# Expert 0's token rows and gates by one-hot products on TensorE, in a two-layer decoder trunk

## The chip, the core and the metric

The kernel runs on one core of one Trainium2 chip. The metric is the device time of one launch in microseconds (us); lower is better. Durations below are those of one profiled execution. Engines are named as in the profile: PE is the matmul engine (PEld its weight loads), DVE, ACT and POOL are the vector, scalar and GpSimd engines, and SP issues DMAs.

## The reference

A trunk of two layers works on 512 tokens of 1024 numbers in float32. Each layer is an attention mixer followed by a mixture of experts, and the change lies in the second part alone:

```python
def hier_moe(xn, ...):            # xn: the stream, normalised
    g_prob = softmax(xt @ w_group + b_group);  g_val, g_idx = top_k(g_prob, 1)
    e_logits = (xt @ w_expert + b_expert)[the chosen group]      # 4 of 16 experts
    e_val, e_idx = top_k(softmax(e_logits), 2);  e_val /= sum(e_val)
    gates[token, expert] = g_val * e_val                         # 0 for all others
    for e in range(16):
        hid = silu(xt @ w_gate[e]) * (xt @ w_up[e])
        out = out + gates[:, e:e + 1] * (hid @ w_down[e])
```

Every token goes to two of sixteen experts, so an expert sees some 64 of the 512 tokens. Its weights are 6 MB: `w_gate` and `w_up` of 1024x512, `w_down` of 512x1024.

## The kernel before

**Precision.** Matmul operands are split into a high and a low part of a shorter float type (`fp32r` in the profile), and a product is three matmuls, high by high, high by low and low by high (`mm3`, L480). ACT writes the high part (`wh`, L191) and DVE the low part (`wl`, L193); some low parts go to POOL. A matmul with both operands in plain float32, such as the one with `twice` in `route_lt` (L827), needs no parts.

**Weight stream.** `Stream` (L115) loads the experts' weights with one DMA of 1 MB per unit from SP's queue. An expert has six units: two of `w_gate`, two of `w_up`, two of `w_down`. Fifteen buffers take turns; a buffer comes free when both of its splits (128x1024 each) are done, and a load also waits until the load three before it has landed. The last two of the fifteen buffers are `h0` and `h1`, in which the stream of token rows `h` stood until the experts began: `row(t)` (L376) is the 128 tokens of tile `t`, `t` = 0 to 3, two tiles to a buffer. Split parts go into six pairs `wh`, `wl`; a pair comes free when the last matmul that reads it is done. `ws.get()` hands out the next pair and splits ahead as far as pairs are free; `ws.get(False)` does not split ahead; `ws.split()` makes one split; `ws.hold()` stops the loads and `ws.go()` lets them go on.

**Routing.** When attention ends, each tile's rows are multiplied by the gain and written to `xn_d` in DRAM (`route_rows`), transposed and multiplied by the routers' weights (`route_logits`, `route_lt`). `select` (L848) works on two tiles at a time (`TS` = 2): DVE compares logits (`beat`, `above`, `ab`), PE counts with `ab` how many tokens stand before each one in its expert's list (`pk`, L881), and DVE forms the place of each token in its two lists (`rs`). `make_lists` (L1278) compares places with slot numbers 1 to 96 (`oneh`, L1284), multiplies by token numbers on PE (`pi`, L1287) and has in `first` and `lists` the token number of each of an expert's 96 slots. `rest` (L915) makes the gate values `ga2` by some 17 small DVE operations and two exponentials, and writes them to `g_d` in DRAM.

**Experts.** `gather` (L1297) fetches an expert's rows from `xn_d` by an indirect DMA that POOL issues, `gates` (L1373) its gate values and row roots from `g_d`. `gathered_t` (L1303) transposes the 96 rows on PE and splits them into `th` and `tl`. `gate_up` (L1309) makes `pg` and `pu`, 24 matmuls of 128x512 each; expert 0's `pg` first takes all 16 matmuls of `th` and then the 8 of `tl`. SiLU and product give `sg`; `hidden_t` transposes and splits it; `down` multiplies by `w_down`, scales by the gates and adds the result into DRAM by an indirect DMA. The two buffers for gathered rows are `xg`.

**Order.** A scheduler orders each engine's instructions by its own estimate of times; the text of the kernel binds it by `behind(lasts)` (L299), which puts everything issued inside behind a named instruction of the same engine, without a wait. Before the change the order at the head of the experts is: `make_lists`, the gathers of experts 0 and 1, 30 matmuls without use (`warm`, L553), all of `rest`, the gates of 0 and 1, four splits, `gathered_t(0)`, gather and gates of expert 2, more splits, and then the loop over the experts.

## Time and profile before

| what | value |
|---|---|
| three timed runs | 1280.27, 1281.66, 1283.16 us (median 1281.66) |
| the profiled execution | 1280.31 us, of which 1278.3 us are the span from the first instruction to the last |
| PE busy | 1213.9 us (95%) |
| DVE, ACT, POOL busy | 1011.3 us (79%), 930.6 us (73%), 366.4 us (29%) |
| TensorE's granted clock, mean | 0.966 of full speed |
| HBM read and written | 260.35 MB, 21.83 MB |

The experts of layer 0 run from about 310 to 600 us and those of layer 1 from about 970 to 1260 us. The granted clock has two levels in this trace, 1.0 (2.4 GHz) and 0.5 (1.2 GHz). A busy PE is not a PE at its peak, since matmuls are pipelined and their ends are modelled; the distance between the starts of two matmuls says more than the duration of one.

### The profile page before, as it was taken

What the parts mean: (1) busy time and instruction counts of PE and PEld (TensorE: products, weight loads), DVE (VectorE), ACT (ScalarE), POOL (GpSimd) and SP (SyncE); (2) the same over time, 40 slices, a digit from 0 to 9 for tenths busy, and PEclk for the clock granted to TensorE, in tenths of its full rate; (3) what the DMA queues carried; (4) which work ended last, traced back from release to release, by engine and by line L of the source; (5) the groups of instructions that cost most, each with busy time, mean ns of one, the idle gap of its engine ahead of it and who ended that gap; (6) DMA issues with size and microseconds to landing.
All of it is one profiled execution on the core that took longest, in us unless ns stands there. A gap on an engine that the chain in (4) does not pass through costs nothing. (4 is left out here: it accounts for less than half of the span.)

```text
span 1278.3 us, 21170 instructions
## 1 busy us (share of the span) xinstructions
PE 1213.9 (95%) x7552; PEld 998.0 (78%) x7552; DVE 1011.3 (79%) x1828; ACT 930.6 (73%) x1697; POOL 366.4 (29%) x337
## 2 busy tenths in 40 slices
PE   8999999997999999999999999997897999999993
PEld 8999999866677777766999999997675777777762
DVE  5678889888998889887767777666587988988883
ACT  6477777655888888877667787767465888888782
POOL 2644441145113433411200011001163133343400
PEclk9999999988999999999999999998697999999997
DMA  6343324859999999995853333337459999999991
GB/s 218 92 106 78 99 59 151 264 183 298 338 349 345 332 331 332 335 350 160 246 144 87 88 100 100 86 103 240 145 190 302 357 346 319 326 322 329 332 357 23
DMA packets 167813, 286.36 MB, mean 224 GB/s; under 512 B 19876, under 2 KB 53807, under 8 KB 167700
## 3 DMA queue, kind: packets, MB, share of 16 engines
q1 hardware_dynamic: 149716, 253.60, 59.1%
q0 software_dynamic: 16496, 30.19, 11.2%
q8 instruction: 63, 1.03, 0.3%
q10 hardware_dynamic: 1488, 1.13, 0.3%
q14 instruction: 50, 0.41, 0.1%
HBM read 260.35 MB, written 21.83 MB: 221 GB/s over the span
## 5 line engine op out<-in xcount | busy, mean ns | idle before, releaser
L193 DVE TENSOR_TENSOR wl<-raw,wh 128x1024 fp32r<-128x1024 f32 (+1 forms) x390 | 472.3, 1241 | 68.1 <-ACT wh L191 64.7
L191 ACT ACTIVATE wh<-raw 128x1024 fp32r<-128x1024 f32 (+1 forms) x456 | 440.7, 988 | 84.9 <-PE pu L483 23.3
L193 POOL TENSOR_TENSOR wl<-raw,wh 128x512 fp32r<-128x512 f32 (+1 forms) x66 | 109.4, 1661 | 184.4 <-ACT wh L191 174.1
L482 PE MATMUL pj<-wl,bh 128*128 128x256 f32 x512 | 145.8, 285 | 0.0
L483 PE MATMUL pj<-wh,bl 128*128 128x256 f32 x512 | 145.6, 286 | 0.0
L481 PE MATMUL pj<-wh,bh 128*128 128x256 f32 x512 | 145.5, 286 | 0.0
L481 PE MATMUL pj<-wh,ah 128*128 128x256 f32 x384 | 110.9, 289 | 1.3 <-ACT wh L191 0.8
L482 PE MATMUL pj<-wl,ah 128*128 128x256 f32 x384 | 111.0, 289 | 1.2 <-POOL wl L193 0.9
L483 PE MATMUL pj<-wh,al 128*128 128x256 f32 x384 | 110.3, 288 | 0.0
L481 PE MATMUL pu<-wh,th 128*96 128x512 f32 x256 | 101.7, 397 | 4.0 <-ACT wh L191 4.0
L482 PE MATMUL pu<-wl,th 128*96 128x512 f32 x256 | 102.5, 400 | 0.0
L481 PE MATMUL pd<-wh,hh 128*96 128x512 f32 x256 | 102.2, 399 | 0.0
L483 PE MATMUL pu<-wh,tl 128*96 128x512 f32 x256 | 101.2, 395 | 0.0
L482 PE MATMUL pd<-wl,hh 128*96 128x512 f32 x256 | 101.1, 395 | 0.0
L483 PE MATMUL pd<-wh,hl 128*96 128x512 f32 x256 | 101.1, 395 | 0.0
L482 PEld LDWEIGHTS pj<-wl,bh 128*128 128x128 f32 x512 | 97.9, 191 | 0.1
L481 PEld LDWEIGHTS pj<-wh,bh 128*128 128x128 f32 x512 | 97.6, 191 | 0.1
L483 PEld LDWEIGHTS pj<-wh,bl 128*128 128x128 f32 x512 | 97.7, 191 | 0.0
L483 PE MATMUL pg<-wh,tl 128*96 128x512 f32 x240 | 97.5, 406 | 0.0
L481 PE MATMUL pg<-wh,th 128*96 128x512 f32 x240 | 96.2, 401 | 0.0
L482 PE MATMUL pg<-wl,th 128*96 128x512 f32 x240 | 95.9, 400 | 0.2 <-DVE wl L193 0.2
L1298 POOL DMA_INDIRECT xg<-xn_d,lists x28 | 50.8, 1813 | 104.1 <-PE xt L527 104.1
(386 smaller groups left out, 2945.7 us busy)
## 6 DMA issues: line engine op xcount, KB each, us to landing
raw<-in_moe_w_gate_dram SPq DMA_DIRECT2D x64, 1024.0 KB
raw<-in_moe_w_up_dram SPq DMA_DIRECT2D x64, 1024.0 KB
raw<-in_moe_w_down_dram SPq DMA_DIRECT2D x64, 1024.0 KB
raw<-in_kv_w_dram SPq DMA_DIRECT2D x12, 1024.0 KB
raw<-in_a_w_in_dram SPq DMA_DIRECT2D x11, 1024.0 KB
raw<-in_b_w_q_dram SPq DMA_DIRECT2D x6, 1024.0 KB
kh<-kh POOLq DMA_DIRECT2D x24, 128.0 KB, 2.9
kl<-kl POOLq DMA_DIRECT2D x24, 128.0 KB, 2.8
```

Source lines behind the costliest of these rows:

```text
L191: nc.scalar.activation(hi[:, o:o + n], src, AF.Copy)
L193: e.tensor_tensor(lo[:, o:o + n], src, hi[:, o:o + n].bitcast(F32), op=ALU.subtract)
L481: nc.tensor.matmul(o, lh, rh, start=start, stop=False)
L482: nc.tensor.matmul(o, lh, rl, start=False, stop=False)
L483: nc.tensor.matmul(o, ll, rh, start=False, stop=stop)
L1298: nc.gpsimd.indirect_dma_start(out=xg[e % XG], out_offset=None, in_=xn_d, in_offset=bass.IndirectOffsetOnAxis(ap=(first if e < XG else lis ...
```

## The change

Expert 0 is no longer gathered from DRAM. For each tile a 0/1 matrix `pick` (128 tokens x 96 slots, float32) is made on DVE from the place of each token in expert 0's list (`rk0`), and plain float32 matmuls `row(t)` by `pick` give the transposed rows of the 96 slots in two banks `picked[0]` and `picked[1]`, each of four 128x96 blocks that sum over the four tiles: 32 products. Eight of them (tiles 0 and 1, first bank) stand behind 24 matmuls without use and ahead of `pk` of the second two tiles; eight (tiles 0 and 1, second bank) behind that `pk`; sixteen (tiles 2 and 3) behind `make_lists`. The split scales by the gain column for column. Expert 0's gate values come out of `ga2` in the same way, by four products (`picked_gates`). Its low part `tl0` takes the buffer `yb` in which results stand later, and `pick` a buffer of `hh`.

The loads into `h0` and `h1` move behind these products, the hold on the loads is gone, and the gathers of experts 1 and 2 follow `make_lists`. `rest` is cut into two pieces that stand between splits, each split and each piece behind the DVE operation before it (`chain`). Expert 0's `pg` takes its eight blocks in two halves and releases two weight pairs after each half; SiLU of expert 0, its transposition and the gates of experts 1 and 2 come later than before.

```diff
-WARM = 60, 30, 20
+WARM = 60, 24, 20
@@ select
-        for t in range(t0, t1):
-            o = pk[:, (t - t0) * 16:(t - t0) * 16 + 16]
+        with behind(r["early"]() if t0 else {}):
+            for t in range(t0, t1):
...
+        r["pkm"] = marks()[mybir.EngineType.PE]
+        with tc.high_priority(100):
+            nc.vector.scalar_tensor_tensor(r["rk0"][:, t0:t1], pk[:, 0:n * 16].rearrange("p (t e) -> p t e", e=NE)[:, :, 0],
+                                           1.0, ab[:, t0:t1, 0], op0=ALU.add, op1=ALU.mult)
@@ rest: yields after the two exponentials and after the write of g_d
+            yield
+            cmax = kt([1, 1], "cmax")
...
@@ moe
-            with behind({sp.engine: sp}, r["sp"]):
-                for i in range(2):
-                    ws.ring(f"h{i}", ...)
-            ws.hold()
+            pick = pm.tile([P, NT, CAP], F32, tag="hh", name="pick", bufs=2)
+            picked = []
+            def pick_ones(t0):
+                with tc.high_priority(100):
+                    for t in range(t0, t0 + TS):
+                        nc.vector.tensor_scalar(pick[:, t], slot16[:, 0:CAP], r["rk0"][:, t:t + 1], None, op0=ALU.is_equal)
+            def pick_rows(t0, gs):
+                for g, k in itertools.product(gs, range(4)):
+                    kc = g * 4 + k
+                    for t in range(t0, t0 + TS):
+                        nc.tensor.matmul(picked[g][:, k * CAP:(k + 1) * CAP], row(t)[:, kc * P:(kc + 1) * P], pick[:, t],
+                                         start=t == 0 and k == 0, stop=t == NT - 1 and k == 3)
+                return marks()[mybir.EngineType.PE]
+            def early():
+                pe = marks()[mybir.EngineType.PE]
+                with behind({pe.engine: pe}):
+                    warm(WARM[1], "pj")
...
+                with behind({pe.engine: pe}):
+                    return {pe.engine: pick_rows(0, [0])}
+            r["early"] = early
+            pick_ones(0)
             route(layer)
+            pick_ones(TS)
+            pe = r["pkm"]
+            with behind({pe.engine: pe}):
+                pe = pick_rows(0, [1])
@@ expert 0's operands and gates
+            def picked_t():
+                th = pm.tile([P, KC, CAP], F32R, tag="th", name="th0", bufs=2)
+                tl = pm.tile([P, KC, CAP], F32R, tag="yb", name="tl0", bufs=1)
+                for g in range(2):
+                    split2s([(th[:, g * 4 + k], tl[:, g * 4 + k], picked[g][:, k * CAP:(k + 1) * CAP],
+                              gffn[layer][:, g * 4 + k:g * 4 + k + 1]) for k in range(4)])
+                    dve = marks()[mybir.EngineType.DVE]
+                    with behind({dve.engine: dve}):
+                        ws.split()
+                return th, tl
+            def picked_gates():
+                pt = ps("sc", "pgx")[0:CAP, 0:NE + 1]
+                for t in range(NT):
+                    nc.tensor.matmul(pt, pick[:, t], r["ga2"][:, t], start=t == 0, stop=t == NT - 1)
+                nc.vector.tensor_copy(gx[0], pt)
@@ gate_up, expert 0
-                        w = [ws.get() for _ in range(4)]
-                        for k in range(2):
-                            for kc in range(KC):
+                        for g in range(2):
+                            w = [ws.get(False) for _ in range(2)]
+                            for k, kc in itertools.product(range(2), range(g * 4, g * 4 + 4)):
...
+                        amid()
@@ the order at the head
-            make_lists()
-            for i in range(XG):
-                gather(i)
-            ws.go(marks()[mybir.EngineType.DVE].name, last_unit[layer] + 1)
...
+            with behind({pe.engine: pe}):
+                make_lists()
             pe = marks()[mybir.EngineType.PE]
             with behind({pe.engine: pe}):
-                warm(WARM[1], "pj")
...
+                pick_rows(TS, range(2))
+            with behind({sp.engine: sp}, r["sp"]):
+                for i in range(2):
+                    ws.ring(f"h{i}", ...)
+            ws.go(None, last_unit[layer] + 1)
+            for i in (1, 2):
+                gather(i)
+            rest = r["rest"]()
...
+            with behind({**r["lsm"], dve.engine: dve}):      # dve: the second oneh
+                for _ in range(2):
+                    ws.split()
+            dve = r["lim"]                                   # lists
+            with behind({dve.engine: dve}):
+                chain(ws.split, also=r["lsm"])
+                tt = picked_t()
+            chain(ws.split, lambda: next(rest), also=r["lsm"])
...
+                    banks = gate_up(0, *tt, lambda: chain(ws.split, ws.split))
+                    chain(lambda: next(rest), ws.split)
...
+                    chain(second_in, first_gates, ws.split)  # gathered_t(1), picked_gates
...
+                    with behind(dve):
+                        sg = activate(0, *banks)
+                        make_last()
+                    for i in (1, 2):
+                        gates(i)
+                    gather(3)
+                    gates(3)
```

## Rows read from the trace of the kernel before

**Rows 1.** Windows, layer 0's head and its steady part; the header names the columns.
```profile
core 0: us, PE busy (x) PEld busy (x) DVE busy (x) ACT busy (x) POOL busy (x), PEclk, DMA share, GB/s
...
299.90:306.70 6.80, 4.42 (x47) 4.23 (x47) 5.76 (x38) 3.85 (x6) 1.98 (x2) 0.51 0.71 240
...
310.12:313.55 3.43, 3.43 (x8) 2.32 (x9) 3.43 (x5) 0.33 (x1) 3.40 (x1) 0.52 0.93 134
...
324.10:326.10 2.00, 0.02 (x1) 0.00 (x0) 2.00 (x4) 2.00 (x4) 0.00 (x0) 1.00 1.02 329
...
327.20:330.60 3.40, 3.40 (x10) 2.21 (x9) 2.49 (x3) 1.28 (x2) 0.00 (x0) 0.51 1.03 323
...
340.00:560.00 220.00, 220.00 (x1050) 156.28 (x1049) 194.78 (x190) 186.50 (x224) 79.22 (x47) 1.00 1.02 338
```

**Rows 2.** Timeline of PE, layer 0: start us, length us, instruction, [idle before <-releaser].
```profile
301.35 0.17 PE L881 MATMUL pk<-ab,strictb 128*128 128x16 bf16 x1
...
303.20 3.36 PE L557 MATMUL warm<-onesb 128*128 128x128 bf16 x30
...
308.99 0.88 PE L527 MATMUL xt<-cm,xg 96*128 96x96 f32 x8 [2.34 <-DMA xg<-xn_d,first]
310.12 0.74 PE L1319 MATMUL pg<-wh,th 128*96 128x512 f32 x1 [0.25 <-ACT th L487]
...
333.19 0.39 PE L483 MATMUL pg<-wh,tl 128*96 128x512 f32 x1
```

**Rows 3.** Timeline of PE, layer 1, the same places.
```profile
960.15 0.17 PE L881 MATMUL pk<-ab,strictb 128*128 128x16 bf16 x1 [0.17 <-DVE ab L875]
...
970.03 0.74 PE L1319 MATMUL pg<-wh,th 128*96 128x512 f32 x1
...
985.52 0.47 PE L481 MATMUL pu<-wh,th 128*96 128x512 f32 x1 [2.01 <-ACT wh L191]
...
992.58 0.39 PE L483 MATMUL pg<-wh,tl 128*96 128x512 f32 x1
```

**Rows 4.** Timeline of POOL, layer 0: gathers of expert 0 and expert 2.
```profile
304.42 1.11 POOL L1298 DMA_INDIRECT xg<-xn_d,first  x1 [8.71 <-DMA raw<-in_moe_w_down_dram]
...
310.14 4.28 POOL L1298 DMA_INDIRECT xg<-xn_d,lists  x1 [3.34 <-PE xt L527]
```

**Rows 5.** Timeline of DVE, layer 0: second one-hot, first six low parts.
```profile
302.24 0.56 DVE L1284 TENSOR_TENSOR oneh<-slot,rs 128x384 f16<-128x384 f16 x1
...
306.62 2.36 DVE L193 TENSOR_TENSOR wl<-raw,wh 128x1024 fp32r<-128x1024 f32 x2
...
308.98 4.61 DVE L193 TENSOR_TENSOR wl<-raw,wh 128x1024 fp32r<-128x1024 f32 x4
313.52 1.00 DVE L488 TENSOR_TENSOR tl<-xt,th 128x384 fp32r<-128x384 f32 x2
```

**Rows 6.** Timeline of PEld: weight loads of plain float32 matmuls, 128 columns each.
```profile
297.69 0.52 PEld L827 LDWEIGHTS lt<-twice,ls 40*128 40x128 f32 x4 [0.62 <-ACT ls L823]
```

**Rows 7.** Timeline of PE: one plain float32 product of 384 columns.
```profile
69.73 0.91 PE L754 MATMUL br<-boh 33*128 33x384 f32 x2
```

**Rows 8.** Groups of DVE by shape: names, shapes, count | busy us, mean ns | idle before.
```profile
L498 DVE SCALAR_TENSOR_TENSOR al<-xt,gcols,ah 128x128 fp32r<-128x128 f32 x32 | 8.7, 342 | 6.1 <-ACT ah L496 6.1
...
L1515 DVE TENSOR_SCALAR ohlast<-slot,last 96x128 fp32r<-96x128 f16 x4 | 1.0, 351 | 0.0
```

**Rows 9.** Timeline of SP: load into `h0` in layer 0, last loads of both layers.
```profile
296.12 0.59 SPq L165 DMA_DIRECT2D raw<-in_moe_w_up_dram  x1
...
569.05 8.46 SPq L165 DMA_DIRECT2D raw<-in_moe_w_down_dram  x4
...
1230.81 8.45 SPq L165 DMA_DIRECT2D raw<-in_moe_w_down_dram  x4
```

**Rows 10.** Timeline of ACT: splits near the end of each layer's experts.
```profile
582.97 5.79 ACT L191 ACTIVATE wh<-raw 128x1024 fp32r<-128x1024 f32 x6
...
1242.21 5.79 ACT L191 ACTIVATE wh<-raw 128x1024 fp32r<-128x1024 f32 x6
```

More of the change, by code (lines that the diff above doesn't have):

```diff
@@ L877, in select @@
         pk = ps(("pv", "sc")[t0 > 0], f"pk{layer}_{t0}")
-        for t in range(t0, t1):
-            o = pk[:, (t - t0) * 16:(t - t0) * 16 + 16]
-            for u in range(t + 1):
-                nc.tensor.matmul(o, strictb if u == t else onesb, ab[:, u, :], start=t == t0 and u == 0,
-                                 stop=t == t1 - 1 and u == t)
+        with behind(r["early"]() if t0 else {}):
+            for t in range(t0, t1):
+                o = pk[:, (t - t0) * 16:(t - t0) * 16 + 16]
+                for u in range(t + 1):
+                    nc.tensor.matmul(o, strictb if u == t else onesb, ab[:, u, :], start=t == t0 and u == 0,
+                                     stop=t == t1 - 1 and u == t)
+        r["pkm"] = marks()[mybir.EngineType.PE]
+        with tc.high_priority(100):
+            nc.vector.scalar_tensor_tensor(r["rk0"][:, t0:t1], pk[:, 0:n * 16].rearrange("p (t e) -> p t e", e=NE)[:, :, 0],
+                                           1.0, ab[:, t0:t1, 0], op0=ALU.add, op1=ALU.mult)
         for k in range(2):
@@ L1285, in make_lists, with make_last @@
                                             r["rs"][:, :, t:t + TS, None].to_broadcast(shape), op=ALU.is_equal)
+                r["ohm"] = marks()[mybir.EngineType.DVE]
                 for i, (t, k) in enumerate(itertools.product(range(NT), range(2))):
                     nc.tensor.matmul(pi, oneh[:, k, t, :], r["mv"][:, k, t, :], start=i == 0, stop=i == 2 * NT - 1)
-                nc.vector.tensor_scalar(first[:, 0:XG], pi[:, 0:XG], OOB, S - 1.0, op0=ALU.add, op1=ALU.min)
+                nc.vector.tensor_scalar(first, pi[:, 0:XG + 1], OOB, S - 1.0, op0=ALU.add, op1=ALU.min)
                 nc.vector.tensor_scalar_add(lists, pi, OOB)
+                r["lim"] = marks()[mybir.EngineType.DVE]
+                r["pi"] = pi
+            def make_last():
                 if layer == 0:
@@ L1299, in gather @@
                     out=xg[e % XG], out_offset=None, in_=xn_d,
-                    in_offset=bass.IndirectOffsetOnAxis(ap=(first if e < XG else lists)[:, e:e + 1], axis=0),
+                    in_offset=bass.IndirectOffsetOnAxis(ap=(first if e <= XG else lists)[:, e:e + 1], axis=0),
                     bounds_check=S - 1, oob_is_err=False)
@@ L1389, in moe @@
-            dve = marks()[mybir.EngineType.DVE]
-            for i in range(XG):
-                gates(i)
-            with behind({**r["lsm"], dve.engine: dve}):
-                for _ in range(4):
-                    ws.split()
-            tt = gathered_t(0)
-            gather(2)
-            gates(2)
-            with behind({**r["lsm"], dve.engine: dve}):
-                ws.ahead()
+                pick_rows(TS, range(2))
+            with behind({sp.engine: sp}, r["sp"]):
+                for i in range(2):
+                    ws.ring(f"h{i}", lambda u, i=i: px.tile([P, 2048], F32, tag=f"h{i}", name=f"raw{u}"), 1)
@@ new lines, in moe, with chain @@
+            ws.go(None, last_unit[layer] + 1)
+            for i in (1, 2):
+                gather(i)
+            rest = r["rest"]()
+            def chain(*fs, also={}):
+                for f in fs:
+                    dve = marks()[mybir.EngineType.DVE]
+                    with behind({**also, dve.engine: dve}):
+                        f()
+            dve = r["ohm"]
+            with behind({**r["lsm"], dve.engine: dve}):
+                for _ in range(2):
+                    ws.split()
@@ L1409, in moe @@
                     tt = gathered_t(e + 1)
-                if hprev is not None:
-                    down(e - 1, *hprev)
+                down(e - 1, *hprev)
                 if e + 3 < NE:
```

59 lines of the change are left out of this document (37 added, 22 removed).

## Prediction

> **What bounds the kernel now.** I read the windows first. Through the experts of a layer PE has no idle time: 220.00 of 220 us between 340 and 560 [rows 1]. There the kernel moves at PE's pace, and what the change can win lies at the two heads, before that state is reached. The same view shows what a head loses: the clock stands at about half from 299.90 to 306.70 and again from 310.12 to 313.55, PE does nothing from 324.10 to 326.10, and the clock is at half once more from 327.20 to 330.60 [rows 1]. The timeline of PE names the waits. After the last count `pk` at 301.35 PE has only lists and matmuls without use to do until expert 0's rows have landed; they are transposed at 308.99 and the first matmul of the experts starts at 310.12 [rows 2]. Layer 1 repeats it: `pk` at 960.15, first matmul at 970.03, and a stall of 2.01 us that a high part from ACT ends at 985.52 [rows 3]. So a head lasts from `pk` to the end of expert 1's `pg`: 301.35 to 333.4 (last start 333.19) and 960.15 to 992.8 [rows 2, 3], about 32 us each. From there on I let everything shift rigidly, unless the weight stream objects.
>
> **The change part by part (layer 0's times).**
>
> *Price of a product.* The trace before has no float32 product of 96 columns, so I bound it. A plain float32 matmul is two instructions, each with its own weight load. Four such loads take 0.52 us at the full clock [rows 6]; with some 0.18 for the last that is (0.52 - 0.18) / 3 = 0.11 us from load to load. The product of 384 columns takes 0.91 us as two instructions [rows 7], 1.2 ns a column and instruction at most, and 0.8 if one load of 0.11 and a tail of some 0.17 are taken off; for 96 columns that is 0.08 to 0.11 us. The load is the longer part, so an instruction costs 0.11 us and a product 0.22; the lower bound is 0.16 (streaming alone), the upper 0.44 (everything at half clock). I take 0.22, since the clock must fall for the other end. The Trainium skill, FP8 and Floating Point Precision, TensorE Precision Notes, counts a true float32 product as four passes through the array. By that rule alone a product of 96 columns would be an estimated 0.16 us and the start below would come 1 us earlier; the rows with their loads decide.
>
> *Up to the first matmul.* The matmuls without use, 30 in 3.36 us at half clock (0.11 each) [rows 2], become 24 and move to 298.3, right after the last logits, where the clock is still full: 0.055 each, 1.3 us, to 299.6. The first `pk` and, on DVE, `rk0` and two comparisons of 128x96 (0.25 each from the four of `ohlast` in 1.0 us [rows 8]) bring the first eight products to 300.6. They take 1.8 us, and the second `pk` stands behind them: 302.4 instead of 301.35, a wait that the change adds. From `pk` to the end of the second one-hot DVE took 302.80 - 301.35 = 1.45 us [rows 2, 5]; `rk0` and two comparisons add 0.7, so the one-hot ends at 304.6, and the next eight products are hidden beside it on PE (302.7 to 304.5). `pi` costs 0.5 us, then sixteen products 3.6: PE is free for experts at 308.7. The first bank is complete at 306.9 and its four high parts cost ACT 1.1 us (as DVE's 128x128 pieces, four in 8.7 / 32 x 4 = 1.1 [rows 8]), so they are no later. Start 308.7 against 310.12: 1.4 us gained. Layer 1 has the same path from a `pk` 658.8 us later, so 967.5 against 970.03 [rows 3]: 2.5 us. What goes with it: gather, landing and transposition of expert 0.
>
> *Clock after the start.* Eight matmuls of 128x512 fall into 310.12 to 313.55, 0.43 us each; at full clock they are begun in half of that, so 8 x 0.2, of which I count 1.4 us for the seven after the first [rows 1], and some 1.0 in layer 1. I expect them back, because PE then has no pause longer than 1 us from 298 on, where before it waited for one-hots and for the gather.
>
> *DVE in the new order.* `chain` makes DVE's order a queue, and a late member holds all behind it. From 304.6: twelve splits for experts 0 and 1 at 1.15 (4.61 / 4 [rows 5]) 13.8, lists 0.3, eight low parts of expert 0 at 0.27 [rows 8] 2.2 (before, two in 1.00 [rows 5]), `rest` 17 x 0.15 (5.76 / 38 [rows 1]) 2.6, expert 1's low parts 1.0: 19.9 us, to 324.5. `rest` no longer stands ahead of the first split (306.62 [rows 5]), which moves up to 304.6. PE needs 66 matmuls of 0.23 (half of 0.43, and a little) from 308.7 to reach expert 1's last split, 15.3 us, with 0.7 for the transposition and 0.9 for the eight instructions of the gates' products: 325.6. Both queues end within 1.1 us of each other. I leave 1 us of stalls: last six matmuls 1.4, transposition of `sg` 0.4, so expert 1's `pg` ends at 328.5 against 333.4. That is the 2.0 us stall and the 1.7 us of half clock behind it (3.40 x 0.5 [rows 1]) less the added products. **Layer 0: -4.9 us.** Layer 1 would reach the same point at 328.5 + 658.8 = 987.3 against 992.8 [rows 3]: -5.5.
>
> *Gates and gathers.* `rest` ends near 320, and SP writes `g_d` then, queued among the weight loads; the gates of expert 1 stand behind that write on POOL, and ahead of the gather of expert 3. Gather 0 took 4.6 us from issue to use (304.42 to 308.99 [rows 2, 4]); with as much for the write, expert 1's gates are there at 329. Its SiLU waits for them, but its product is needed only after `pu` of expert 1 and `down` of 0, some 10 us on: no cost. The gathers of experts 1 and 2 now follow the lists at 305.5, into the first splits of DVE. Gather 0, beside small operations, took POOL 1.11 us; the one that began beside splits took 4.28 [rows 4]. With 4.28 instead of 1.11 expert 1's rows land 7.8 us after 305.5, at 313.3; they are needed near 318. No cost, with 5 us as cover; without it each us late stops PE. The Trainium skill, SBUF — State Buffer, SBUF: two separate sides, says that some DVE operations lock POOL out of a port pair, so that its DMAs' descriptors come late; that speaks against this place for a gather, and the two rows agree with it.
>
> *The weight stream.* SP issued the loads into `h0` and `h1` at 296.12 and just after [rows 9]. Now the two wait for the products that read `row(t)`: 304.5 and 308.7. The stream has some 6 us more to carry from 308.7 on (2.7 us a load, 8.46 for four issues [rows 9]) and one gather less. At the head of layer 0 loads waited for free buffers anyway, so I put the net delay at 1 us; in layer 1, where the stream is slower at the end (below) and I trust that cover less, at a load's time, 3. What can it bear? The last four loads are issued 2.7 us apart, the fourth only when the first has landed: 577.1 and 1238.9 [rows 9]. ACT splits that first one as the third load of a run of six splits, at 584.9 and 1244.1 [rows 10]: 7.8 and 5.2 us spare. Layer 0 keeps its 4.9 (7.8 - 1 = 6.8). Layer 1 has 5.2 - 3 = 2.2 spare to the split, and up to 5.5 if the stream is not late at all; I take the middle, **-3.8 us.**
>
> **Sum.** 4.9 + 3.8 = 8.7 us off the profiled execution: 1280.31 - 8.7 = 1271.6. The median of the shown runs stands 1.35 above that execution, so I forecast 1281.66 - 8.7 = 1273.0. A difference of 0.2% (2.6 us) is about what a measurement of this kernel can tell from none.
>
> **The rivals.**
>
> *The stream takes it back.* If the two delayed loads put the stream 5 us behind in each layer, 2.8 and 0.2 us of spare time are all that is gained at the ends: -3.0, 1278.7. For it: the last loads leave only 5.2 us in layer 1 [rows 9, 10]. Against it: early loads waited for splits, and those come earlier now. Chance 0.17.
>
> *DVE's queue.* If low parts of expert 0 wait for PE's banks, the splits behind them in `chain` wait too. A wait of 2 us, and one of 2 in `rest` for ACT's exponentials, leave 0.9 us of layer 0 and 1.5 of layer 1: -2.4, 1279.3, hardly to be told from no change. Chance 0.13.
>
> *Slower: the products run at half clock.* In the trace before the clock fell at 299.90 [rows 1], in the middle of where the products now stand. If it still does and does not come back before the experts, 32 products cost 0.44 instead of 0.22, 7 us, and lists 0.4 more: start at 316.1, 6.0 late. The stall of 2.0 and its 1.7 us of half clock still go, expert 0's half clock at the start remains and the gates' products cost 0.9: +3.2 a layer, 1288. It decides from some 20 of the 32 products on: 20 x 0.22 = 4.4 us, the mean gain of a layer. The Trainium skill, TensorE: Matmul & The Clock Gate, Why this matters for your kernels, says that pauses between bursts of matmuls drop the clock; the fall at 299.90 behind a pause agrees. Chance 0.20.
>
> **How the numbers follow.** Forecast 0.50, the stream 0.17, DVE's queue 0.13, half clock 0.20. The range reaches from the full gain in both layers with the cheap product (10.4 + 1 a layer: 1269, and 1 below for the runs' spread, 1268) over the two smaller gains and no change to 1283, where a quarter of the slow case lies inside. Faster by over 0.2%: forecast and most of the stream case, 0.66. Within 0.2%: DVE's queue and a little of the stream, 0.14. Slower: 0.20.
>
> **What would show it.** Right: products 0.11 us an instruction; clock 1.0 from 298 to 330; the first `pg` matmul near 308.7 and 967.5; no stall of 2 us near 324; `pg` of expert 1 ending 4 to 6 us earlier counted from the last logits; last splits less than 5 us behind their loads. Wrong: a granted clock of 0.5 between 300 and 309; splits of the late experts that wait for a load; DVE idle between the first and the sixth split; a first `pg` after 311.

## The result, and the profile after

The change made the kernel slower. Its median is 1294.99 us over 14 runs (1283.00 to 1305.62), beside 1281.72 for the kernel before over 14 runs (1277.54 to 1284.05): a ratio of 1.0087, 95% interval 1.0062 to 1.0111. The ratio leaves out the two slowest runs of the change (1305.04 and 1305.62 us), which count as slow ones; by the medians it is 1.0104. I had forecast 1273.0 and a range that ended at 1283. Besides the median the spread has grown, from 6.5 to 22.6 us; that is a finding of its own, as will be seen. The profiled execution took 1298.10 us, its span is 1296.3 against 1278.3.

**The head does what was forecast.** First the windows of the kernel after, layer 0 (us, PE busy, PEld busy, DVE busy, ACT busy, POOL busy, granted clock, DMA share, GB/s):

```profile
297.00:308.00 11.00, 9.99 (x112) 9.77 (x113) 9.81 (x45) 7.05 (x11) 1.39 (x1) 1.00 0.23 69
308.00:328.00 20.00, 19.16 (x95) 13.58 (x95) 18.51 (x47) 15.31 (x22) 4.20 (x3) 1.00 1.02 330
340.00:560.00 220.00, 210.17 (x985) 147.30 (x984) 191.44 (x177) 176.26 (x215) 132.26 (x48) 0.98 1.03 343
380.00:400.00 20.00, 15.06 (x62) 9.98 (x61) 12.09 (x10) 14.21 (x18) 8.69 (x6) 0.83 0.92 298
```

The first two stand where [rows 1] had a clock of 0.51 and 0.52 and a PE without work: now the clock is 1.00 throughout. The third line is the surprise. In the stretch in which PE had been busy for 220.00 of 220 us [rows 1], it is idle for 9.83, and POOL is busy for 132 instead of 79 us with one instruction more. The fourth shows one place of it, with 5 us of idle PE and a clock of 0.83.

PE's timeline after, layer 0 and then layer 1:

```profile
302.35 0.17 PE L882 MATMUL pk<-ab,strictb 128*128 128x16 bf16 x1
302.38 2.00 PE L1286 MATMUL xp<-pick,h 128*128 128x96 f32 x16
...
304.61 3.79 PE L1286 MATMUL xp<-pick,h 128*128 128x96 f32 x32
308.19 0.46 PE L1378 MATMUL pg<-wh,th 128*96 128x512 f32 x1
...
327.34 0.40 PE L483 MATMUL pg<-wh,tl 128*96 128x512 f32 x1
...
978.80 0.17 PE L882 MATMUL pk<-ab,strictb 128*128 128x16 bf16 x1
...
984.64 0.45 PE L1378 MATMUL pg<-wh,th 128*96 128x512 f32 x1
...
1003.80 0.40 PE L483 MATMUL pg<-wh,tl 128*96 128x512 f32 x1
```

To compare kernels whose earlier parts shift, I count from the start of the last logits' matmul `lt` of a layer. From there expert 0's `pg` began after 12.07 us (layer 0) and 12.71 (layer 1) before, and begins after 10.47 and 10.36 now. The last `pg` matmul of expert 1 began after 35.1 and 35.3 us [rows 2, 3], and begins after 29.6 and 29.5 now: 5.5 and 5.7 us of gain, a little more than forecast. In layer 0 all of it is gone by the fifth expert: PE needs the layer's 56th split 98.6 us after the last `lt` before, and 104.1 us after it now. In layer 1 1.6 us are still left there, and none at the end of the layer.

**Where it goes.** POOL, SP, ACT and DVE just behind that point, in the kernel after:

```profile
317.91 1.76 POOL L1340 DMA_INDIRECT xg<-xn_d,lists  x1 [7.16 <-DVE ga L955]
331.04 7.69 POOL L1439 DMA_INDIRECT gx<-g_d,lists  x1 [11.38 <-DMA g_d<-ga]
339.04 0.97 POOL L1439 DMA_INDIRECT gx<-g_d,lists  x1 [0.30 <-issue]
...
348.09 1.98 POOL L1434 DMA_INDIRECT h_d<-yb,lists  x1 [5.54 <-ACT yb L1431]
...
362.32 16.96 POOL L1434 DMA_INDIRECT h_d<-yb,lists  x1 [3.07 <-ACT yb L1431]
```

```profile
322.15 0.37 SPq L956 DMA_DIRECT2D g_d<-ga  x1
```

```profile
343.12 0.68 ACT L1399 ACTIVATE sg<-pg,gx 96x512 f32<-96x512 f32 x1 [6.84 <-DMA gx<-g_d,lists]
```

```profile
327.80 6.89 DVE L193 TENSOR_TENSOR wl<-raw,wh 128x1024 fp32r<-128x1024 f32 x6
...
337.80 0.55 DVE L488 TENSOR_TENSOR tl<-xt,th 128x384 fp32r<-128x384 f32 x1
343.84 0.75 DVE L1400 SCALAR_TENSOR_TENSOR sg<-pu,gx,sg 96x512 f32<-96x512 f32 x1 [5.49 <-ACT sg L1399]
```

The gates of expert 1 are gathered at 331.04, when `g_d` has landed, and issuing that gather takes POOL 7.69 us; the next takes 0.97. The long one ends at 338.73, 0.4 us after DVE has done its last low part at 338.35 and stands still. ACT had reached the SiLU of expert 1 at 336.28 and waits there for 6.84 us with all its splits behind it, DVE waits for ACT for 5.49, and PE then for 2.25. The kernel before issued its gathers of gates, those of experts 0 to 3, here (two of the four, POOL):

```profile
314.73 0.97 POOL L1374 DMA_INDIRECT gx<-g_d,lists  x1 [0.30 <-issue]
...
317.28 0.96 POOL L1374 DMA_INDIRECT gx<-g_d,lists  x1 [0.30 <-issue]
```

and its DVE stood still at that very time, from 314.58 to 317.67, waiting for a high part from ACT:

```profile
317.67 6.90 DVE L193 TENSOR_TENSOR wl<-raw,wh 128x1024 fp32r<-128x1024 f32 x6 [3.09 <-ACT wh L191]
```

The change has no such standstill between 321.11 and 338.35: my own sum laid 19.9 us of DVE's work end to end at the head.

It does not end with the gates. Groups of POOL between 340 and 620 us (busy us, mean ns), the results' scatter-adds and the gathers of gates, after:

```profile
L1434 POOL DMA_INDIRECT h_d<-yb,lists x15 | 79.7, 5315 | 92.4 <-ACT yb L1431 92.4
...
L1439 POOL DMA_INDIRECT gx<-g_d,lists x14 | 24.5, 1751 | 4.3 <-issue 3.7 <-DVE wl L193 0.6
```

and the same stretch before:

```profile
L1369 POOL DMA_INDIRECT h_d<-yb,lists x15 | 27.0, 1802 | 94.5 <-ACT yb L1366 94.5
...
L1374 POOL DMA_INDIRECT gx<-g_d,lists x12 | 12.4, 1033 | 3.7 <-issue 3.0 <-DVE wl L193 0.3 <-DMA raw<-in_moe_w_gate_dram 0.3
```

Before, no scatter-add took over 1.97 us. After, five of fifteen take 16.96, 9.76, 9.48, 11.56 and 10.01. `yb` has one buffer, so ACT cannot write the next result until the scatter-add has read it. ACT's waits over the whole run of the kernel after (total us, times, longest):

```profile
ACT yb L1431 <- DMA h_d<-yb,lists: 29.1, 5, 10.3
...
ACT sg L1399 <- DMA gx<-g_d,lists: 12.4, 2, 6.8
```

Neither pair stands among ACT's waits before. The sum: from the last `lt` to the last `pd`, layer 0 took 301.39 us before and 316.17 after, layer 1 301.36 and 302.36, and the stretch between them 357.87 and 360.39: 14.8 + 1.0 + 2.5 us, which is all of the 18.0 by which the spans differ (what lies outside is 0.3 us shorter). In layer 0 PE waits for 2.25 us behind the gather of the gates, and for 4.42, 2.53 and 3.98 us behind scatter-adds that took long.

**Theory F**, which the experiments test: while DVE works through low parts without a break, an instruction of POOL beside it can starve, until DVE has caught up with ACT and stands still for a moment. Before, the stall at the head gave POOL that moment, just when the gates were issued. The change fills it with work.

### The profile page after: what moved, and what is told of

Same layout as the page of the kernel before. It is cut to its first block, busy times and chain, and to the rows that moved or that the text cites. A ratio compares the mean times of both kernels' runs of the same rounds, so it can differ in the third digit from the quotient of the medians.

```text
span 1296.3 us, 21423 instructions
## 1 busy us (share of the span) xinstructions
PE 1222.4 (94%) x7668; PEld 1004.8 (78%) x7668; DVE 1017.6 (78%) x1854; ACT 928.5 (72%) x1709; POOL 445.2 (34%) x333
## 5 line engine op out<-in xcount | busy, mean ns | idle before, releaser
L193 DVE TENSOR_TENSOR wl<-raw,wh 128x1024 fp32r<-128x1024 f32 (+1 forms) x390 | 477.6, 1265 | 59.7 <-ACT wh L191 58.4
L1434 POOL DMA_INDIRECT h_d<-yb,lists x15 | 79.7, 5315 | 92.4 <-ACT yb L1431 92.4
```

The lines of the kernel that those rows point to most:

```text
L193: e.tensor_tensor(lo[:, o:o + n], src, hi[:, o:o + n].bitcast(F32), op=ALU.subtract)
L1434: nc.gpsimd.indirect_dma_start(out=sums[layer], out_offset=bass.IndirectOffsetOnAxis(ap=lists[:, e:e + 1], axis=0), in_=yb, in_offset=None ...
```

## The experiments

Each expectation stands as it was written before its runs, with the letters that the theories had then; the text behind it says what it decided. Times are medians; ratios are to the kernel before on the same chip.

**e1, gates early.** If lateness were the fault (theory A), writing `g_d` ahead of the splits should cure it.

```diff
-            chain(ws.split, lambda: next(rest), also=r["lsm"])
+            chain(ws.split, also=r["lsm"])      # and both pieces of rest, gates(1), gates(2) right behind `lists`
```

> The changed kernel with the gates' operations (rest), the write of g_d and the gathers of experts 1 and 2's gates back ahead of the third split; the picked rows and the rest of the order stay. Theory A (the late gates start the trouble: the gather of expert 1's gates comes into DVE's dense splits, ACT waits for it, and POOL's scatter-adds then starve): ACT's SiLU of expert 1 waits for nothing of the gates, scatter-adds take 1.5 to 2 us each, the first pg comes some 1 us later than 308.2 because DVE's low parts stand behind rest; 1275 to 1279. Theory B (the earlier start alone does it: DVE has more splits to catch up with, whatever the gates do): scatter-adds of 8 us and more stay, 1289 to 1297.

Measured: 1289.20 us, ratio 1.0056 [1.0030, 1.0081]. The write goes out 12 us earlier (SP), but the gather of expert 1's gates, now at 323.18, takes longer still (POOL):

```profile
310.03 0.64 SPq L956 DMA_DIRECT2D g_d<-ga  x1
```

```profile
323.18 11.57 POOL L1439 DMA_INDIRECT gx<-g_d,lists  x1 [13.27 <-DVE last L1336]
335.05 0.97 POOL L1439 DMA_INDIRECT gx<-g_d,lists  x1 [0.30 <-issue]
```

```profile
333.82 0.55 DVE L488 TENSOR_TENSOR hl<-ht,hh 128x384 fp32r<-128x384 f32 x1
341.13 2.36 DVE L193 TENSOR_TENSOR wl<-raw,wh 128x1024 fp32r<-128x1024 f32 x2 [6.76 <-ACT wh L191]
```

DVE worked without a break from 321.5 to 334.4; the gather ends at 334.75. Being 8 us earlier does not cure it, and ACT's SiLU of expert 1 waits for 8.09 us, PE for 7.07. Theory B, whose time this is, has missed too: it wanted scatter-adds of 8 us and more, and none took over 5.07. In layer 1 the gathers behind expert 1's took 7.17 (gates) and 5.82 us (rows), and PE waited for 6.07 for the rows. Together with e2 lateness falls as the cause.

**e2, gates late in the kernel before.** A second table, written after expert 1's low parts, serves the gates of experts 1 and on.

```diff
+   nc.vector.tensor_copy(late, r["ga2"]);  nc.sync.dma_start(g2_d..., late);  gates(1); gates(2)
...
-   out=gx[e % 4], out_offset=None, in_=g_d,
+   out=gx[e % 4], out_offset=None, in_=g2_d if e else g_d,
```

> The kernel before, with the one part done alone: expert 0's gates as they were, the gates of experts 1 and up read from a second table that is written only after expert 1's low parts, and gathered after that. Theory A: the gather of expert 1's gates takes over 4 us, ACT's SiLU of expert 1 waits several us, scatter-adds of over 5 us follow; 1287 to 1297. Theory B: one wait of a few us at most in each layer, scatter-adds stay near 1.9 us; 1281 to 1285.

Measured: 1273.17 us, 0.9934 [0.9908, 0.9959]. The gathers run at 336 us, later than in the kernel after, and none starves (POOL, then DVE at the same time):

```profile
336.37 0.97 POOL L1375 DMA_INDIRECT gx<-g_d,lists  x1 [12.81 <-DMA g_d<-late]
337.64 0.98 POOL L1375 DMA_INDIRECT gx<-g_d,lists  x1 [0.31 <-issue]
```

```profile
336.55 1.23 DVE L193 TENSOR_TENSOR wl<-raw,wh 128x1024 fp32r<-128x1024 f32 x1 [0.19 <-ACT wh L191]
338.03 1.22 DVE L193 TENSOR_TENSOR wl<-raw,wh 128x1024 fp32r<-128x1024 f32 x1 [0.25 <-ACT wh L191]
```

DVE waits for ACT for about 0.2 us ahead of each split here, and that seems to be enough. The layers take 300.72 and 301.09 us, as before, so late gates alone cost nothing; both theories' ranges lie above this time. That the kernel got faster comes from the stretch between the layers (351.06 instead of 357.87), where nothing was edited: PE stands at half clock there for 30.7 us instead of 37.5, and its waits of over 0.3 us come to 13.5 us instead of 17.4. Why is not shown.

**e3 and e4, without scatter-adds**, in the kernel after and the kernel before.

```diff
+                if e % NE == 0:
                     nc.gpsimd.indirect_dma_start(out=sums[layer], ..., in_=yb, ..., compute_op=ALU.add)
```

> The changed kernel without the scatter-adds of experts 1 to 15 (expert 0's stays; the sums of the other experts are left out). Both theories put the persistent loss into scatter-adds that POOL cannot issue beside DVE's splits, so without them the stalls of 2.5 to 4.4 us from 380 us on must go: only the head's gain less the wait of 2.3 us at expert 1 is left, 4 to 8 us under the kernel before without the same scatter-adds. Theory C (the loss comes from the weight stream or from another engine): the kernel stays 8 us or more above the kernel before without them.

> The kernel before without the scatter-adds of experts 1 to 15, as the partner of the run above. In the trace of before they take 1.6 to 2.0 us and nothing waits for them, so 1278 to 1282 by all theories.

Measured: 1257.94 and 1254.91 us, 0.9827 [0.9794, 0.9859] and 0.9783 [0.9754, 0.9812]. Without scatter-adds the 13 us between the kernels shrink to 3.0, which four runs of each can hardly tell from none. e4 is some 25 us below what I had expected, and hardly any of that lies in the layers: 17.4 us lie behind the last product of layer 1, where the kernel before still has a scatter-add to issue and to wait for, and 6.2 in the stretch between the layers. The change's layers then take 299.96 and 300.46 us against 301.52 and 300.79: a gain of 1.6 and 0.3, far from the 5 of the head, because the gates' gather still starves (6.93 us, PE idle for 2.53). So the starved scatter-adds carry most of the loss, and the starved gather eats the gain; e10 shows the second half.

**e5, PE later.** 92 matmuls without use ahead of the first `pg` set PE back, so that expert 1's last `pg` matmul begins 35.1 us after the last `lt`, as before; if the loss were a matter of PE running ahead of DVE (theory D), it should vanish.

```diff
+                    with behind({pe.engine: pe}):
+                        warm(92, "pj")
```

> The changed kernel with 92 more matmuls without use between the picks and expert 0's first matmul: 80 of them hold PE for 4.4 us a layer (0.055 us each), 12 lie in its wait for the one-hots. Nothing else is changed. Theory D (PE now starts so early that it stands right behind the splits: DVE then has none ahead and runs without a gap, and POOL, which needs a gap on DVE to issue a gather or a scatter-add, starves; ACT waits for what POOL issues): with PE later DVE gets its lead of over 2 us back, POOL's issues stay under 4.5 us, and the kernel gets faster although 9 us of idle work were added: 1278 to 1285. Rival A (late gates or the picks themselves do it, whenever PE starts): the added 9 us come on top, 1299 to 1306.

Measured: 1301.29 us, 1.0143 [1.0103, 1.0183], in rival A's range; theory D falls. The chained order of DVE follows PE, so the two keep their phase: the gates' gather takes 9.05 us, ACT waits 9.0, PE 8.42. The scatter-adds behind it take 3.32 us at most, so it seems that which of them starve depends on the phase that the first wait leaves behind.

**e6, a turn for each scatter-add.** DVE's low part of each hidden tile waits for a POOL memset that stands behind the scatter-add.

```diff
+                r["turn"] = inst(nc.gpsimd.memset(turn_, 0.0)).name      # behind the scatter-add, on POOL
...
+                    tc.add_manual_dep(marks()[mybir.EngineType.DVE], r.pop("turn"), ...)   # hl waits for it
```

> The changed kernel with a turn for POOL: behind each scatter-add POOL writes a small tile, and DVE's low part of the next hidden tile waits for that write, so DVE makes a gap when POOL still has the scatter-add to issue. Theory D: scatter-adds end within 4.5 us, the waits of ACT for yb go, the wait of ACT for expert 1's gates stays; from the last logits to the last product of a layer 299 to 302 us in both layers (316.2 and 302.4 in the profile of the change, 301.4 before), 1279 to 1284 in all. Rival E (DVE has no time left, so a gap given to POOL is lost by the splits): PE waits for low parts instead, 1288 to 1297.

Measured: 1293.39 us, 1.0081 [1.0048, 1.0113], in rival E's range. The waits for `yb` are gone and no scatter-add takes over 5.4 us, but most take 4.7 to 5.4 and the standstill recurs in every such expert (POOL):

```profile
418.49 5.38 POOL L1439 DMA_INDIRECT h_d<-yb,lists  x1 [5.78 <-ACT yb L1436]
...
436.83 5.37 POOL L1439 DMA_INDIRECT h_d<-yb,lists  x1 [5.79 <-ACT yb L1436]
```

The period is 18.34 us where it was 17.72 in the kernel before, some 0.6 us an expert; over 15 experts that would be about 9 us a layer, and the layers take 312.09 and 312.59 us. That DVE has no time left, as rival E says, fits this.

**e7 and e8, expert 1's gates by one-hots too**, so that no gather is due at the dense time; the comparisons on DVE. e8 has e6's turns as well.

```diff
+   nc.vector.tensor_copy(rk1, rk[:, :, 1])
...
+   nc.vector.tensor_scalar(pick1[:, t], slot16[:, 0:CAP], rk1[:, t:t + 1], None, op0=ALU.is_equal)
...
+   nc.tensor.matmul(pt, pick1[:, t], r["ga2"][:, t], start=t == 0, stop=t == NT - 1)
+   nc.vector.tensor_copy(gx[1], pt)
-                    for i in (1, 2):
-                        gates(i)
+                    gates(2)
```

> The changed kernel with expert 1's gates taken by one-hot products too (four more comparisons and one copy on DVE, eight instructions on PE), so that ACT's SiLU of expert 1 waits for no gather. Theory D: the wait of 2.25 us at expert 1 and the half clock behind it go, but DVE is as dense as before, so scatter-adds of over 5 us remain in layer 0: 1284 to 1294. Rival A (the wait for the late gates is what shifts ACT and DVE against POOL): without that wait the scatter-adds stay under 2.5 us, 1272 to 1278.

> Both of the last two edits. Theory D: both losses go, what is left is the head's gain less a lead of PE that DVE can't follow: 296 to 300 us from the last logits to the last product of a layer, 1271 to 1279. Rival E: PE waits for low parts, 1284 to 1294.

Measured: e7 1287.55 us (ten runs, 1278.63 to 1291.57), 1.0036 [1.0011, 1.0062]; e8 1291.98, 1.0087 [1.0055, 1.0119]. The SiLU of expert 1 no longer waits, but six more DVE operations in the dense stretch cost 3 us by the tenth split, and in e7 two scatter-adds still starve (8.82 and 10.47 us); its profile shows an execution of 1278.88 us, one of the three shortest of the ten. e8 lies in rival E's range, 4.4 us above e7.

**e9 and e10, the same at no cost.** Expert 1 gets a copy of expert 0's gates, and e10 leaves out the scatter-adds of experts 1 to 15 besides.

```diff
+                        nc.vector.tensor_copy(gx[1], gx[0])
-                    for i in (1, 2):
-                        gates(i)
+                    gates(2)
```

> The changed kernel without the gather of expert 1's gates: expert 1 is given a copy of expert 0's gates (one copy of 96x17 on DVE), so its weights are left out of the result. Theory F (POOL can issue a gather or a scatter-add only when DVE pauses, and DVE pauses only when it has caught up with ACT; the change fills the pause at the head in which the gates' gathers were issued): without a wait of ACT PE keeps 4 to 5 us of the head's gain up to the second expert, and loses some of it later where DVE lies behind ACT and a scatter-add starves; 296 to 305 us from the last logits to the last product, 1274 to 1290. Theory G (DVE's queue at the head ends no earlier than before, so PE must give its gain back in waits for low parts, whatever POOL does): PE waits for low parts for some 4 us within the first three experts, and both layers take 299.5 us or more.

> The same, and without the scatter-adds of experts 1 to 15 as well (both parts are left out of the result). Theory F: nothing that POOL issues is waited for, so the head's gain stays: 295.5 to 298 us from the last logits to the last product in both layers (300.0 and 300.5 with the gather, 301.5 and 300.8 in the kernel before without scatter-adds), 1243 to 1251. Theory G: 299.5 to 301.5 in both, 1254 to 1259.

Measured: e9 1277.17 us, 0.9978 [0.9961, 0.9995], with one scatter-add of 10.01 us left in layer 0 (PE idle for 4.54); e10 1244.07 us, 0.9730 [0.9712, 0.9749], 10.8 below e4. e10 is the cleanest reading of the head: with nothing on POOL to starve, its layers take 296.54 and 296.10 us, 5.0 and 4.7 less than e4's. I had forecast 4.9 and 5.5 for the heads.

**e11, e14, the comparisons on POOL**, which stands idle around 318 us; e14 is the same kernel again. Beside e7 a second thing differs: the four products and the copy move to a later place, into expert 1's `pg`.

```diff
-   nc.vector.tensor_scalar(pick1[:, t], ...)
+   nc.gpsimd.tensor_scalar(pick1[:, t], slot16[:, 0:CAP], rk1[:, t:t + 1], None, op0=ALU.is_equal)
```

> The changed kernel with expert 1's gates by one-hot products, the comparisons on POOL, which has nothing to do then, instead of on DVE. Theory F: ACT's wait goes and DVE's queue is no longer than in the change, so the second expert starts 3.5 to 5 us earlier than before, where the run with the comparisons on DVE had 1.6; scatter-adds of over 5 us still come now and then; 1275 to 1288. Theory G: the same as with DVE, 1284 to 1292.

> The kernel with expert 1's comparisons on POOL once more, for a second profile of it: 1270 to 1275. If its gain is the edit's, the two layers together are again 2 to 5 us shorter than before; if the 4.5 us that the stretch between the layers gave in the first profile came by chance, that stretch lies elsewhere within 351 to 360 now.

Measured: 1271.65 us, 0.9939 [0.9921, 0.9957], and 1272.45 us, 0.9945 [0.9929, 0.9961]: faster than both kernels (as e2 is). On POOL the comparisons take 2.97 us, and the group of the scatter-adds (layer 0) is almost back to that of before:

```profile
318.30 2.97 POOL L1373 TENSOR_SCALAR pick<-slot,rk 128x96 f32<-128x96 f16 x4
...
333.72 6.85 POOL L1455 DMA_INDIRECT gx<-g_d,lists  x1 [11.26 <-DMA g_d<-ga]
```

```profile
L1450 POOL DMA_INDIRECT h_d<-yb,lists x15 | 30.8, 2050 | 86.2 <-ACT yb L1447 85.9 <-issue 0.3
```

The gather at 333.72 starves as the kernel after's did, but it is now expert 2's and nobody waits for it. e14's two layers are together 3.8 us shorter than before, within the 2 to 5 expected, and its stretch between the layers took 352.91 us where e11's took 353.36 and before's 357.87 and 358.23: that part came again too, though nothing was edited there. The windows of e11 show PE at full work where the kernel after stood still:

```profile
340.00:360.00 20.00, 20.00 (x95) 14.16 (x94) 19.32 (x21) 17.83 (x22) 11.26 (x6) 1.00 1.05 355
...
380.00:400.00 20.00, 20.00 (x96) 14.15 (x95) 18.21 (x19) 17.05 (x21) 8.05 (x6) 1.00 1.00 344
```

**e12, two low parts of the head to POOL** on top of e11, to relieve DVE.

```diff
-   "pool" if 24 <= i[0] < 84 and (i[0] % 6, k) == (3, 0) else None
+   "pool" if (24 <= i[0] < 84 and (i[0] % 6, k) == (3, 0)) or (i[0] in (5, 7) and k == 0) else None
```

> The same, and two of the low parts of the first two experts on POOL instead of DVE (2.3 us off DVE's queue, some 5 us onto POOL's, which is idle there). Theory F: DVE catches up with ACT two splits earlier, so the scatter-adds of the first 100 us stay under 4 us; 1272 to 1284. Rival H (a low part on POOL holds DVE up as long as it takes itself): nothing gained or worse, 1284 to 1292.

Measured: 1283.04 us, 1.0035 [1.0013, 1.0057]. POOL's timeline, then DVE's:

```profile
321.49 2.40 POOL L193 TENSOR_TENSOR wl<-raw,wh 128x1024 fp32r<-128x1024 f32 x1
...
325.50 11.68 POOL L193 TENSOR_TENSOR wl<-raw,wh 128x1024 fp32r<-128x1024 f32 x1 [1.61 <-ACT wh L191]
```

```profile
329.24 5.75 DVE L193 TENSOR_TENSOR wl<-raw,wh 128x1024 fp32r<-128x1024 f32 x5
```

So it is not a matter of DMAs alone: POOL's own subtraction of the same shape takes 2.40 us once and 11.68 the other time (2.39 and 2.47 in layer 1), and ends 2.2 us, about its own length, after DVE's last low part at 334.99. PE is idle for 5.21. The time lies in theory F's range, but the two splits did not help.

**e13, one pause.** The test that theory F stands or falls by: the kernel after with one standstill added. One low part of DVE a layer, at some 332 us in layer 0, waits for a POOL memset behind the gather of expert 1's gates.

```diff
+                    gates(1)
...
+                        ws.turn = first_split + 18, inst(nc.gpsimd.memset(turn, 0.0)).name
...
+                        gates(2)
...
+                if self.turn and self.turn[0] == self.n_split:
+                    self.tc.add_manual_dep(inst(low), self.turn[1], ...)
```

> The changed kernel with one pause for POOL a layer and nothing else: behind the gather of expert 1's gates POOL writes a small tile, and one low part on DVE, the second ahead of expert 0's hidden tile (332.3 in the profile of the change), waits for that write. Theory F: the gather takes under 3 us instead of 7.7, ACT's SiLU of expert 1 waits under 2 us instead of 6.8, and although DVE was made to stand still for some 1 us the kernel gets faster: at the fifth expert PE is 2 to 4.5 us earlier than before (5.5 later in the change), 1273 to 1285. Rival (the pause costs the splits what it gives POOL): PE waits for low parts as long as it had waited for the hidden tile, 1290 to 1297.

Measured: 1279.22 us (12 runs), 0.9991 [0.9976, 1.0006]. POOL, DVE and ACT at that place:

```profile
331.69 1.96 POOL L1446 DMA_INDIRECT gx<-g_d,lists  x1 [12.05 <-DMA g_d<-ga]
333.65 0.12 POOL L1506 MEMSET turn<- 96x2 f32 x1
```

```profile
333.80 2.36 DVE L194 TENSOR_TENSOR wl<-raw,wh 128x1024 fp32r<-128x1024 f32 x2 [0.99 <-POOL turn L1506]
```

```profile
338.43 0.69 ACT L1406 ACTIVATE sg<-pg,gx 96x512 f32<-96x512 f32 x1 [0.67 <-DMA gx<-g_d,lists]
```

DVE stands still for 0.99 us; the gather takes 1.96 instead of 7.69, the SiLU waits for 0.67 instead of 6.84, and the kernel is 15.8 us faster than the change by its median (some 12 by the ratios). In layer 1 the gather takes 2.14 us. Nothing was made shorter or left out. One scatter-add of layer 0 still starves (10.02 us at 557.47).

**e15 and e16, both kernels again**, one profile each.

> The kernel before once more, for a second profile: both layers 301 to 302 us from the last logits to the last product, scatter-adds under 2.1 us, and the stretch between the layers anywhere within 351 to 360.

> The changed kernel once more, for a second profile. Theory F: the gather of expert 1's gates again takes over 6 us and ACT's SiLU of expert 1 waits over 5 us in both layers, since that part follows from the order; the scatter-adds of over 5 us come at other experts than in the first profile, since those hang on how far DVE lies behind ACT at that moment.

Measured: 1280.45 and 1295.33 us. The kernel before repeats itself: layers of 301.74 and 301.34. The kernel after does not: 312.17 and 310.23, with the gates' gather starved in both layers again (6.90 and 8.52 us; 7.69 and 7.12 in the first profile), and the scatter-adds at other experts (8.98, 9.00, 11.55 and 10.02 us in layer 0, 13.63 and 11.94 in layer 1) than in its first profile. The program is the same, so the order on each engine is the same; which instruction meets a dense stretch differs from run to run. This is what a spread of 22.6 us looks like from the inside.

## Why the prediction was wrong, step by step

- *Price of a product: right.* 32 instructions in 3.79 us, 0.118 each and 0.24 a product, against 0.22 forecast. The 0.16 estimated from the four passes of the Trainium skill (FP8 and Floating Point Precision, TensorE Precision Notes) was too low here.
- *First `pg`: right.* 308.19 against 308.7; counted from the last `lt`, 1.6 and 2.35 us of gain against 1.4 and 2.5.
- *Clock after the start: right.* 1.00 from 297 to 328. With it falls the rival of half clock, the one that I held for a slower kernel at 1288.
- *DVE in the new order: right up to expert 1's `pg`.* 5.5 and 5.7 us of gain against 4.9 and 5.5. The rival of DVE's queue had the right engine and the wrong damage: DVE was not too slow for PE, it left POOL no opening.
- *"Gates and gathers ... no cost": wrong, and the first of the two steps at which the forecast failed.* I had counted the gates of expert 1 there at 329 with "some 10 us" in hand: 4.6 us for the write of `g_d` and 4.6 for the gather. The write went out at 322.15 and had landed only at 331.04, after 8.9 us; that alone would have cost next to nothing, as e13 shows, where the SiLU waits for 0.67. But the gather then took 7.69 us, landed near 343, and the SiLU of expert 1 waited for 6.84. The "no cost" was right about PE's need for the product and wrong about ACT: its queue holds the high parts for every engine's next work behind that SiLU. The evidence was among my rows: a gather that took 4.28 us beside splits, where another took 1.11 [rows 4]. I moved that number to the gathers of experts 1 and 2 and priced a single delay at 3 us; for the gates I took the quiet 4.6. I never asked what opened the door for the gathers that were quick: the first three gates' gathers of before began in DVE's standstill of 3.09 us, which the sum filled with work without asking who had used it.
- The Trainium skill, SBUF — State Buffer, SBUF: two separate sides, which I had set against the gathers' place, names the right two engines, but not this operation. It blames late descriptors on DVE's two-port modes, and says, under Who interferes with whom, that a probe with `tensor_tensor`, which is what a low part is, showed no stalled DMA. The runs show otherwise: the waits lie beside just these operations. The size differs as well: it says that whoever starts first holds the ports for the whole instruction, by which POOL would wait for one low part, an estimated 1.2 us from DVE's rows. The traces show waits through six to twelve of them, 7.69, 11.57 and 16.96 us.
- *The weight stream: the gain at a layer's end is smaller, as I feared, but not by the stream.* Once POOL's trouble is out of the way, e11 and e14 show the layers at 299.56 and 300.55, 299.86 and 299.09 us: a gain of 1.5 to 2.3 in three of four and 0.8 in the other, against the 5 at the head. At the 56th split of layer 0 PE has 4.2 us of lead over the kernel before (94.4 us after the last `lt` against 98.6), and e11's last run of six splits begins 1.8 us earlier, counted so (at 582.32 against 582.97 [rows 10]). Of what is lost between, 1.7 us are waits of PE for DVE, which the kernel before does not have there (PE, e11):

```profile
550.77 0.52 PE L1422 MATMUL ht<-cm,sg 96*128 96x96 f32 x4 [1.17 <-DVE tl L488]
551.81 0.47 PE L482 MATMUL pd<-wl,hh 128*96 128x512 f32 x1 [0.52 <-DVE wl L193]
```

e11's layer 1 and both layers of e14 have the same two waits, and e10, with the scatter-adds left out, keeps all of its gain. In e11 and e14 no layer's splits wait for loads for more than 0.3 us in all, so the rival that I gave 0.17 is not what took the gain back. Why DVE is late there is open.
- *"From there on I let everything shift rigidly": wrong, the second step, and in microseconds the larger.* It rested on 220.00 busy us of 220 [rows 1]. That line shows that PE was never kept waiting, not that there was room: the order on each engine in the steady part is the same in both kernels, and it runs in two ways, with scatter-adds of 2 us or with a third of them at 10. What decides seems to be where the breaks in DVE's low parts lie beside POOL's instructions; that the two ways differ in nothing else was not tested.

**What is shown, and what is not.** Shown: beside DVE's low parts of 128x1024 that follow each other without a break, an instruction on POOL, its own subtraction too, can take several times as long as alone, and a break made on purpose cures it. At its place in the change's order the gather of expert 1's gates took 6.90 to 10.49 us in all ten layers of five profiles (the change twice, e3, e5, e6); with e13's pause it took 1.96 and 2.14, and the kernel is again as fast as the one before (0.9991).

Theory F is too narrow in one point: a standstill is not the only break that helps. The starved scatter-adds of layer 0 of the kernel after ended 1.3 to 1.4 us after a standstill began, and one of under 0.2 us at 485.5 was enough for the scatter-add of 475.25. But the gates' gather of layer 1 ended at 1014.94 beside a DVE that went on working (POOL, then DVE):

```profile
1007.82 7.12 POOL L1439 DMA_INDIRECT gx<-g_d,lists  x1 [11.64 <-DMA g_d<-ga]
```

```profile
1014.00 0.55 DVE L488 TENSOR_TENSOR tl<-xt,th 128x384 fp32r<-128x384 f32 x1
1014.47 1.22 DVE L193 TENSOR_TENSOR wl<-raw,wh 128x1024 fp32r<-128x1024 f32 x1
```

That is 0.4 us after the short low part `tl`, whose operand `xt` PE has written, and the gather of layer 0 ended as long after the same `tl` (338.35). So the standstill of 5.49 us there, which is itself the result of ACT's wait for the gather, need not be what let the gather end. Of the 77 gathers and scatter-adds of over 5 us in the experts of all eighteen profiles 26 ended without a standstill of DVE of over 0.1 us.

Dense work does not always starve POOL, either: in the kernel before the gathers at 318.54 and 321.16 went through in 1.19 and 1.99 us beside six low parts with no gap on record. Over all profiles, of the instructions that began with more than 3 us of unbroken low parts of weights ahead, 47 of 52 scatter-adds took over 2.5 us, but only 28 of 87 gathers of gates and 5 of 47 gathers of rows. What lets the others pass is open. Open, too, is the stretch between the layers, between 348 and 360 us over these profiles, whose edits lie elsewhere: of the 6.4 us by which e11's profile is shorter only 2.6 lie in its two layers and 4.5 there, and e2 owes it 6.8. A second buffer for `yb`, which would loosen ACT from the scatter-adds, was not tried.

## What to carry to other kernels

Before filling an engine's standstill, look at what the other engines do during it: here it was when POOL could issue. A gather or scatter on POOL beside dense two-operand work on DVE can take ten microseconds instead of one or two (here nearly every scatter-add and a third of the gates' gathers were slowed), and whoever waits for it in order (here ACT, with a single result buffer) hands the delay to everyone. If it bites, move the small work off POOL's critical gathers, as e11 does, or give POOL one deliberate opening where a late issue hurts, as e13 does; a pause in every round cost more than it saved here (e6).

## What the runs showed of the hardware that was not expected

- POOL's gathers and scatter-adds beside DVE's low parts took from about 1 us to 16.96 us in the kernel after; the same subtraction on POOL took 2.40 and 11.68 us (e12).
- One pause of DVE a layer, 0.99 us in layer 0, took the median from 1294.99 to 1279.22 us (e13).
- One program with one order on each engine ran layer 1 in 302.36 us in one execution and in 310.23 in another, while the kernel before stayed within 0.4 us.
